# Dilated-attention values of two units of heads by seven block products instead of eight, with block sums made by transfers

## The chip, the cores and the metric

The kernel runs on one core of one Trainium2 chip. The metric is the device time of one execution in microseconds. Before the change it is 734.18 us, the median of three runs (733.82 to 734.69).

## The reference, cut to what matters

A four-layer encoder works on 256 tokens of width 1024, all in float32: an even layer (neighbourhood attention beside latent attention), an MLP, an odd layer (dilated attention), a second MLP. The change lies in the odd layer:

```python
def odd_mixer(xn, w_in, w_o, cos_f, sin_f):
    hcat = (xn @ w_in).reshape(b, s, DIL_GROUPS, 3, DIL_HEADS, HEAD_DIM)   # 3 groups; q, k, v; 16 heads of 64
    q = apply_rope(hcat[:, :, :, 0], cos_f, sin_f)
    k = apply_rope(hcat[:, :, :, 1], cos_f, sin_f)
    v = hcat[:, :, :, 2]
    return dilated_attention(q, k, v) @ w_o
```

Each head attends in three groups of keys (steps 1, 4 and 16), and the three results are mixed by their softmax denominators. Only the way in which `v` is computed changes, and with it one addition of the rotary embedding.

## The kernel before

**Precision.** A float32 matrix is carried as two parts of the type float32r: `hi` is the value cast by ScalarE, `lo` the remainder, taken by VectorE (`split`, L205 and L206). A product is three matmuls, hi·hi, hi·lo and lo·hi (`mm3`, L209 to L211).

**Weights.** One list, `specs`, holds every piece of weight in the order in which it is used. `weight()` (L196) gives the next piece; before that it lets `load_weight` run 4 pieces ahead (a transfer from SP into one of 4 rotating buffers `raw`, L151) and `split_piece` 2 pieces ahead (casts into `whi` by ScalarE and remainders into `wlo` by VectorE, in parts of a piece; 3 buffers of each). In the MLPs one block of a piece is a sum: GpSimd (POOL) copies a block and issues a transfer that adds two more blocks of HBM to it in SBUF (L144, L145).

**The odd layer.** The 16 heads are taken as 8 units of two heads. A unit has three pieces for queries and keys (`w_oqk`, 1024 KB each) and two for the values of its three groups (`w_ov`, 768 KB each). `qk_steps` makes 12 steps: step (b, f, half) is 8 matmuls of a 512-column and a 256-column form (L927, L928). After each f ScalarE and VectorE clear the bank (L934, L935); after each b follows the rotary embedding (`rope`, L939): four transfers on SP swap 32-row blocks into `sw` (L942), VectorE multiplies twice (L947, L948) and adds (L950 for b = 0; L953 for b = 1 and 2, into `q12` and `k12`). `all_values` then makes the values in 4 steps: two halves of 128 tokens times two halves of the width, 48 matmuls of 128x384, whose results VectorE (L904, into `v0`) and ScalarE (L907, L908, into `v12`) scale out of PSUM.

**What sets the order.** `weave` (L220) writes one unit's steps (main) and, spread between them, the attention of the unit before it (side): its scores (L218, L981), softmax (L992 to L997), four transposes of the probabilities (L1004, L1006), and the `mix` of the unit before that (L1019, L1024). From unit 2 on this is the loop at L1043. A scheduler that runs when the program is built then orders each engine's queue, and may take a split or a matmul of a later step first. Every queue runs in its order: an instruction that waits holds up all that stand behind it on its engine. Four PSUM banks are called `acc` and four `w`.

Of the kernel before, what the change touches and what calls it, by code (L numbers as in the profile page):

```python
# [43 lines left out]
WPARTS = 4  # L45
NORM_PRIO = 300
# [3 lines left out]
def trunk(ctx, tc, a, out):  # L50
# [54 lines left out]

    specs = []

    def plan(name, n):
        for j in range(a[name].shape[0]):
            specs.append((a[name][j], n, WPARTS, False))  # L110

    def plan_mlp(layer):
        up = [(a["w1"][layer, j], WCH, 2, False) for j in range(16)]
        down = [(a["w2"][layer, j], WCH, 2, j < 14) for j in range(16)]
# [19 lines left out]
    state = {"loaded": 0, "split": (0, 0), "used": 0, "pool": None, "parts_done": None}  # L134

    def load_weight(pieces=1, before=lambda i: None):
        j = state["loaded"]
        src, n, _, seven = specs[j]
# [8 lines left out]
        raw = wraw.tile([P, WCH], F32, tag="raw", name="raw")  # L147
# [5 lines left out]
        state["loaded"] = j + 1  # L153
# [5 lines left out]
    def split_piece(eng=None):  # L159
        j, i = state["split"]  # L160
        _, _, n, seven = specs[j]
# [11 lines left out]
        return split(hi, lo, raw, eng)  # L173
# [116 lines left out]
    def column(r, t):  # L290
        return r[:, t:t + 1]
# [578 lines left out]
    def odd(op, xT, s, late):  # L870
# [15 lines left out]
        def value_steps(d):  # L886
# [15 lines left out]
            def out(i):  # L902
                pq, ri = acc[i], column(r[0], i)
                nc.vector.tensor_scalar(d["v0"][:, i, :], pq[:, 0:P], ri, None, ALU.mult)  # L904
                for c in range(2):
                    rows = slice(64 * c, 64 * c + 64)
                    nc.scalar.activation(d["v12"][64:P, 2 * i + c, :], pq[rows, P:2 * P], AF.Copy, scale=ri[rows])  # L907
                    nc.scalar.activation(d["v12"][0:64, 2 * i + c, :], pq[rows, 2 * P:3 * P], AF.Copy, scale=ri[rows])  # L908

            return [lambda i=i, h=h: gemm(i, h) for i in range(NT) for h in range(2)], [lambda i=i: out(i) for i in range(NT)]  # L910

        def qk_steps(d, wide=True):
# [26 lines left out]
            def rope(b, pq):  # L939
# [6 lines left out]
                sw = sw.rearrange("p (f n) -> p f n", f=2)  # L946
                nc.vector.tensor_tensor(r1, pq.rearrange("p (f n) -> p f n", f=2), cosT.unsqueeze(1).broadcast_to([P, 2, T]), op=ALU.mult)  # L947
# [208 lines left out]
```

## Time and profile before

| | |
|---|---|
| median of three runs | 734.18 us |
| the profiled execution | 734.39 us, its span 732.6 us |
| TensorE (PE) busy | 723.4 us, 99% |
| VectorE (DVE) busy | 623.7 us, 85% |
| ScalarE (ACT) busy | 521.8 us, 71% |
| GpSimd (POOL) busy | 75.8 us, 10% |
| granted clock of TensorE, mean | 0.999 |
| units 1 to 7 of the odd layer begin at | 315.0, 343.4, 373.6, 403.3, 433.0, 462.7 and 492.5 us |

Times count from the start of the span. A row of a group ends with its busy time, the mean of one instruction in ns, and the idle time of its engine just before such instructions with what ended it. A row of a list in order of time begins with start and duration in us; back-to-back instructions overlap, so the spacing of two starts is what one costs its engine. A stage's row gives its length and then for each engine the busy time in it.

### The profile page before, as it was taken

Reading aid. Unit: us, or ns where it says so; the run is one execution under the profiler, and the core shown is the slowest. Engines: PE = TensorE matmul, PEld = TensorE weight load, DVE = VectorE, ACT = ScalarE, POOL = GpSimd, SP = SyncE. Lnnn points to the kernel's source line nnn. Section 1 sums busy time; section 2 is a strip of 40 time slices with the busy share of each in tenths; the row PEclk is TensorE's granted clock in tenths of the full one; section 3 lists DMA queues with packets and bytes.
Section 4 is the critical chain, followed back from the end, with each engine's and each line's share of the span. In section 5 each row is a group of like instructions: output and inputs, shape, how many; then the busy total and the mean of one; then the engine's idle time right before and its main releaser. Section 6 shows DMA issues by size and latency. Waiting matters only on the chain.

```text
span 732.6 us, 13831 instructions
## 1 busy us (share of the span) xinstructions
PE 723.4 (99%) x5234; PEld 661.0 (90%) x5234; DVE 623.7 (85%) x1188; ACT 521.8 (71%) x985; POOL 75.8 (10%) x73
## 2 busy tenths in 40 slices
PE   9999999999999999999999999999999999999995
PEld 6988899999999998989899899998999999999995
DVE  6888859999999959988777888788759998999956
ACT  7778968767767756877676766867658766776851
POOL 0100002224212000000000000000003132222000
PEclk9999999999999999999999999999999999999999
DMA  8773338799888644664655456455558797898601
GB/s 314 278 260 135 116 115 216 214 283 249 264 265 231 218 160 166 216 211 149 223 181 176 167 187 212 167 187 200 204 190 201 242 271 217 259 272 241 217 32 59
DMA packets 38212, 149.56 MB, mean 204 GB/s; under 512 B 5121, under 2 KB 6657, under 8 KB 29057
## 3 DMA queue, kind: packets, MB, share of 16 engines
q1 hardware_dynamic: 30240, 133.71, 51.6%
q0 software_dynamic: 7616, 14.68, 12.1%
q8 instruction: 41, 0.67, 0.4%
q10 hardware_dynamic: 288, 0.28, 0.1%
q14 instruction: 27, 0.21, 0.1%
HBM read 142.10 MB, written 1.05 MB: 195 GB/s over the span
## 4 chain that ended last, share of the span: by engine, by line
PE 82%; issue 10%; DVE 4%; ACT 1%; DMA 1%; POOL 0%; POOLq 0%; ACTq 0%; DVEq 0%
PE acc L927 11%; PE acc L209 10%; PE acc L210 9%; PE w L209 9%; PE w L210 9%; PE acc L211 9%; PE w L211 9%; PE acc L928 5%; PE w L218 1%; PE w L1004 1%; DVE wlo L206 1%; PE acc L1019 1%; PE w L806 1%; DMA sum<-in_w 1%; PE w L820 1%
## 5 line engine op out<-in xcount | busy, mean ns | idle before, releaser
L206 DVE TENSOR_TENSOR wlo<-raw,whi 128x512 fp32r<-128x512 f32 (+3 forms) x360 | 297.3, 847 | 51.9 <-ACT whi L205 51.8
L205 ACT CAST whi<-raw 128x512 fp32r<-128x512 f32 (+3 forms) x360 | 253.5, 746 | 87.2 <-PE w L210 58.9
L210 PE MATMUL w<-xx,whi 128*128 128x256 f32 x528 | 149.6, 283 | 0.2
L211 PE MATMUL w<-xx,wlo 128*128 128x256 f32 x528 | 149.3, 283 | 0.0
L209 PE MATMUL w<-xx,whi 128*128 128x256 f32 x528 | 148.9, 283 | 0.0
L927 PE MATMUL acc<-xx,whi 128*128 128x512 f32 x336 | 122.1, 404 | 0.0
L210 PEld LDWEIGHTS w<-xx,whi 128*128 128x128 f32 x528 | 101.2, 192 | 1.7 <-DVE xx L246 0.6
L209 PEld LDWEIGHTS w<-xx,whi 128*128 128x128 f32 x528 | 101.0, 192 | 1.1
L211 PEld LDWEIGHTS w<-xx,wlo 128*128 128x128 f32 x528 | 101.2, 192 | 0.0
L928 PE MATMUL acc<-xx,wlo 128*128 128x256 f32 x336 | 94.4, 281 | 0.0
L144 POOL COPY sum<-sum 128x512 f32<-128x512 f32 x28 | 39.3, 1417 | 463.6 <-DMA sum<-in_w 406.6
L927 PEld LDWEIGHTS acc<-xx,whi 128*128 128x128 f32 x336 | 63.1, 188 | 14.2
L928 PEld LDWEIGHTS acc<-xx,wlo 128*128 128x128 f32 x336 | 63.5, 189 | 0.0
L209 PE MATMUL acc<-whi,xx 128*128 128x384 f32 (+2 forms) x160 | 55.9, 351 | 0.0
L210 PE MATMUL acc<-wlo,xx 128*128 128x384 f32 (+2 forms) x160 | 55.4, 346 | 0.0
L211 PE MATMUL acc<-whi,xx 128*128 128x384 f32 (+2 forms) x160 | 54.9, 343 | 0.0
L205 ACT CAST hh<-h 128x896 fp32r<-128x896 f32 (+1 forms) x32 | 28.9, 904 | 24.5 <-DVE h L382 23.7
L209 PE MATMUL w<-whi,hh 128*128 128x512 f32 (+1 forms) x108 | 42.1, 390 | 0.0
L210 PE MATMUL w<-wlo,hh 128*128 128x512 f32 (+1 forms) x108 | 41.5, 384 | 0.0
L211 PE MATMUL w<-whi,hl 128*128 128x512 f32 (+1 forms) x108 | 41.2, 382 | 0.0
L206 DVE TENSOR_TENSOR hl<-h,hh 128x896 fp32r<-128x896 f32 (+1 forms) x32 | 34.8, 1087 | 0.0
L206 DVE TENSOR_TENSOR suml<-sum,sumh 128x1024 fp32r<-128x1024 f32 x28 | 34.4, 1229 | 0.0
(232 smaller groups left out, 1545.6 us busy)
## 6 DMA issues: line engine op xcount, KB each, us to landing
raw<-in_w SPq DMA_DIRECT2D x36, 1024.0 KB, 5.5
raw<-in_w_oqk SPq DMA_DIRECT2D x24, 1024.0 KB, 4.9
raw<-in_w SPq DMA_DIRECT2D x28, 768.0 KB, 4.8
sum<-in_w POOLq DMA_DIRECT2D x28, 512.0 KB, 7.9
raw<-in_w_ov SPq DMA_DIRECT2D x16, 768.0 KB, 4.4
sum<-in_w SPq DMA_DIRECT2D x28, 256.0 KB, 5.9
sw<-qk SPq DMA_DIRECT2D x84, 64.0 KB, 2.4
raw<-in_w_oe SPq DMA_DIRECT2D x4, 1024.0 KB, 5.9
```

Source lines behind the costliest of these rows:

```text
L144: nc.gpsimd.tensor_copy(out=sums[:, 1, :], in_=sums[:, 0, :])
L205: a = nc.scalar.copy(hi, src).ins
L206: return a, (eng or nc.vector).tensor_tensor(lo, src, hi.bitcast(F32), op=ALU.subtract).ins
L209: nc.tensor.matmul(o, sh, mh, start=first, stop=False)
L210: nc.tensor.matmul(o, sh, ml, start=False, stop=False)
L211: nc.tensor.matmul(o, sl, mh, start=False, stop=last)
L218: nc.tensor.matmul(o[j], y[pb, 0, ts], z[pb, 1, :], start=n == 0, stop=n == 2)
L806: nc.tensor.transpose(pt[:, b * P:(b + 1) * P], pp[:, b // 2, (b % 2) * P:(b % 2 + 1) * P], ident)
L820: nc.tensor.matmul(pvo[64 * j:64 * j + 64, 0:P], v[:, kk, h * 64:(h + 1) * 64], pts[:, 2 * j + kk, :], start=kk == 0, stop=kk == NT - 1)
L927: nc.tensor.matmul(two(pq), wh[:, ws], xT[:, k], start=k == 0, stop=False)
L928: nc.tensor.matmul(pq[:, T:2 * T], wl[:, ws], xh[:, k, :], start=False, stop=k == KT - 1)
L1004: nc.tensor.transpose(pt[:, b * P:(b + 1) * P], pp[:, at:at + P], ident)
```

## The change

The units 2 to 7 are taken as three pairs (2, 3), (4, 5) and (6, 7). For a pair the values are a product of 2 x 2 blocks: two halves of the tokens, two halves of the width (even and odd blocks of 128 features), two units. Written plainly that is eight block products of 12 matmuls each. Now it is seven (`pair_values`): P1, Q7, P2 and Q6 in the even unit of a pair, and Q4, Q5 and Q3 at the end of the odd unit, with sums of blocks on both sides.

- The sums of the token side are made once (`combine`, four calls: two woven into unit 1, two into unit 2): four ACT copies of 128x256 in two calls, three VectorE subtractions and a split each, into `combh` and `combl`.
- The weights are now four blocks for each pair (`w_op`, 768 KB each, b11 to b22; the same numbers in another layout). The sums of the weight side are made by transfers that POOL issues and that add a block of HBM onto a buffer `raw`. One buffer is held for a pair: it is loaded with b12, gets b22 added (for Q7); once it has been split for Q7 it gets b11 added (for Q6), and once it has been split for that, b21 (for Q4). Q5's piece is b11 with b12 added. While this lasts the other pieces rotate through 3 buffers.
- Value pieces are split in 2 parts of 768 columns (before: 4 of 384), seven pieces to a pair instead of four.
- The seven results are combined in two SBUF tiles `t` and `v` and in PSUM: ScalarE copies one, VectorE does eight operations of 128x384 to a pair, four of them into a scratch `c`, from which ScalarE scales into `v0` and `v12` (`place`).
- In `rope` for b = 1 of units 1 to 7 the product goes straight into `q12`, and a transfer of POOL adds `sw` to it.

```diff
 VCH = 4 * 384                                   # new
     for u in range(8):
-        ov = [(a["w_ov"][u, j], 4 * 384, WPARTS, False) for j in range(2)]
+        if u < 2:
+            ov = [piece(a["w_ov"][u, j], VCH, WPARTS) for j in range(2)]
+        else:
+            b11, b12, b21, b22 = (a["w_op"][u // 2 - 1, f] for f in range(4))
+            ov = [piece(b11, VCH, 2), piece(b12, VCH, 2, add=b22, held=True, then=b11),
+                  piece(b21, VCH, 2), piece(None, VCH, 2, held=True, then=b21)] if u % 2 == 0 else \
+                 [piece(None, VCH, 2, held=True), piece(b11, VCH, 2, add=b12), piece(b22, VCH, 2)]
         specs.extend(oqk + ov if u else ov + oqk)
...
+    def raw_tile(j, held=False):
+        if not held:
+            state["raw"] = (state["raw"] + 1) % (RAWBUFS - (summed[0] <= j <= summed[-1]))
+        return wraw.tile([P, WCH], F32, tag=f"raw{RAWBUFS - 1 if held else state['raw']}", name="raw", bufs=1)
...
+        if held:
+            if src is None:
+                parts[j] = [state["held"], None, None]
+                return
+            state["held"] = raw_tile(j, True)
...
+        if add is not None:
+            nc.gpsimd.dma_start(raw[:, 0:n], add, accum_op=ALU.add)
...
-        return split(hi, lo, raw, eng)
+        done = split(hi, lo, raw, eng)
+        if i == n - 1 and then is not None:
+            nc.gpsimd.dma_start(parts[j][0][:, 0:width], then, accum_op=ALU.add)
+        return done
...
+        def combine(b):
+            g, e = scratch([4, P], "g"), scratch([4, P], "e")
+            for f in range(2):
+                k = 2 * b + f
+                nc.scalar.activation(g[:, 2 * f:2 * f + 2, :], x[:, k, :].rearrange("p (t n) -> p t n", t=2), AF.Copy,
+                                     scale=gains[:, 2 * KT + k:2 * KT + k + 1])
+            nc.vector.tensor_tensor(e[:, 2:4, :], g[:, 1:2, :].broadcast_to([P, 2, P]), g[:, 0:4:3, :], op=ALU.subtract)
+            nc.vector.tensor_tensor(e[:, 1, :], g[:, 0, :], e[:, 3, :], op=ALU.subtract)
+            nc.vector.tensor_tensor(e[:, 0, :], g[:, 2, :], e[:, 1, :], op=ALU.subtract)
+            split(*(z[:, b] for z in comb), e)
+
+        def pair_values(first):
+            t, v = (op.tile([P, 384], F32, tag=n, name=n, bufs=1) for n in ("pt", "pv"))
+            plain, sums = {"P1": (0, 0), "P2": (1, 0), "Q4": (1, 1)}, {"Q3": 0, "Q6": 1, "Q7": 2, "Q5": 3}
+            def product(n):
+                wh, wl = weight()
+                pq = bank("acc")[:, 0:384]
+                for b in range(KT // 2):
+                    ws = slice(b * 384, b * 384 + 384)
...
+                    mm3(pq, a_h, a_l, wh[:, ws], wl[:, ws], b == 0, b == KT // 2 - 1)
+                return pq
+            def place(d, i, pq, other, op):
+                c = scratch([384], "c")
+                nc.vector.tensor_tensor(c, pq, other, op=op)
+                nc.scalar.activation(d["v0"][:, i, :], c[:, 0:P], AF.Copy, scale=column(r[0], i))
+                strided_values(d, i, c)
+            def p1():
+                nc.scalar.copy(t, product("P1"))
+            def q7():
+                nc.vector.tensor_tensor(v, product("Q7"), t, op=ALU.subtract)
+            def p2():
+                place(first, 0, product("P2"), t, ALU.add)
+            def q6():
+                pq = product("Q6")
+                nc.vector.tensor_tensor(t, pq, t, op=ALU.subtract)
+                nc.vector.tensor_tensor(v, pq, v, op=ALU.add)
...
+            return [p1, q7, p2, q6], lambda second: [q4, lambda: q5(second), lambda: q3(second)]
...
+                if b == 1 and wide:
+                    r1 = d["q12"]
...
+                elif b == 1 and wide:
+                    nc.gpsimd.dma_start(r1, sw, accum_op=ALU.add)
...
+        main[4:4], main[10:10] = [lambda: combine(0)], [lambda: combine(1)]
...
+            if u % 2 == 0:
+                now, later = pair_values(nd)
+            else:
+                now = later(nd)
+            weave(main + now, side + [lambda: mix(6, d, "acc")] if u == 7 else side)
```

Three places show how the queues change. **POOL between the two MLPs**, before (`rstd` belongs to the norm ahead of the odd layer, `sum` to the MLPs):

```order
L145 DMA sum<-in_w 128x2x512
L269 TENSOR_TENSOR rstd<-ms,mhalf 128x2
L144 COPY sum<-sum 128x512
L145 DMA sum<-in_w 128x2x512
L144 COPY sum<-sum 128x512 x2
```

and now, from unit 1 to unit 4 (L180 is a sum of a piece that is being loaded, L203 one that follows a split; `raw_4380` is the held buffer of the first pair, `raw_5183` of the second; `raw_4786` is Q5's piece):

```order
L300 TENSOR_TENSOR rstd_3578<-ms_3582,mhalf_92 128x2
L1057 DMA q12_3463<-sw_4014 128x512
L180 DMA raw_4380<-in_w_op 128x1536
L203 DMA raw_4380<-in_w_op 128x1536
L1057 DMA q12_4204<-sw_4449 128x512
L203 DMA raw_4380<-in_w_op 128x1536
L180 DMA raw_4786<-in_w_op 128x1536
L180 DMA raw_5183<-in_w_op 128x1536
L1057 DMA q12_4629<-sw_4852 128x512
L203 DMA raw_5183<-in_w_op 128x1536
L1057 DMA q12_5022<-sw_5243 128x512
```

POOL had nothing to do in the odd layer and now issues 19 adding transfers there: 4 to a pair and 7 of `q12`.

**VectorE in unit 2**, after the softmax of unit 1, before (`qk` clears an `acc` bank, `pts` takes transposed probabilities):

```order
L206 TENSOR_TENSOR wlo<-raw,whi 128x384
L947 TENSOR_TENSOR r_4333<-qk,cosT 128x512
L935 TENSOR_TENSOR qk<-acc,low 128x256
L206 TENSOR_TENSOR wlo<-raw,whi 128x384 x2
L1006 COPY pts<-w 128x384
L935 TENSOR_TENSOR qk<-acc,low 128x256
L206 TENSOR_TENSOR wlo<-raw,whi 128x384 x3
```

and now (with what each row waits for; `DMASW` is a transfer of POOL):

```order
L1037 TENSOR_TENSOR qk_4222<-acc_4334,low_4360 128x256 [waits Activation_49]
L958 TENSOR_TENSOR e_4344<-g_4343,e_4344 128x128 [waits DVE_49]
L959 TENSOR_TENSOR e_4344<-g_4343,e_4344 128x128 [waits DVE_49]
L237 TENSOR_TENSOR wlo_4523<-raw_4380,whi_4522 128x768 [waits DMASW7_49,PE_49,Activation_49]
L237 TENSOR_TENSOR combl_3454<-e_4344,combh_3453 128x512 [waits Activation_49]
L1051 TENSOR_TENSOR r1_4364<-qk_4222,cosT_3443 128x512
L1037 TENSOR_TENSOR qk_4393<-acc_4394,low_4411 128x256 [waits Activation_49]
L237 TENSOR_TENSOR wlo_4523<-raw_4380,whi_4522 128x768
```

The split of the held buffer waits for a sum by POOL and stands ahead of the row that clears the bank `acc_4394` of the queries.

**SP in unit 2**, before (`sw` are the swaps of the rotary embedding):

```order
L151 DMA raw<-in_w_oqk 128x2048 x2
L942 DMA sw<-qk 32x512 x4
L151 DMA raw<-in_w_oqk 128x2048
L942 DMA sw<-qk 32x512 x4
L151 DMA raw<-in_w_ov 128x1536
L942 DMA sw<-qk 32x512 x4
```

and now (unit 2 and the first loads of unit 3):

```order
L178 DMA raw_4549<-in_w_oqk 128x2048
L178 DMA raw_4380<-in_w_op 128x1536
L178 DMA raw_4571<-in_w_oqk 128x2048
L1044 DMA sw_4363<-qk_4222 32x512 x4
L1044 DMA sw_4449<-qk_4393 32x512 x4
L1044 DMA sw_4513<-qk_4466 32x512 x4
L178 DMA raw_4600<-in_w_oqk 128x2048
L178 DMA raw_4786<-in_w_op 128x1536
L178 DMA raw_4861<-in_w_op 128x1536
```

The loads of a unit stood one by one between the swaps; now they stand in groups ahead of and behind them. The held buffer is the fourth `raw`, so its load waits until the third piece of queries and keys of unit 2, which lay in it, has been split.

More of the change, by code (lines that the diff above doesn't have):

```diff
@@ L45 @@
 WPARTS = 4
+VCH = 4 * 384
 NORM_PRIO = 300
@@ L106, in trunk, with piece @@
     specs = []
+    def piece(src, n, parts, seven=False, add=None, held=False, then=None):
+        return src, n, parts, seven, add, held, then
     def plan(name, n):
         for j in range(a[name].shape[0]):
-            specs.append((a[name][j], n, WPARTS, False))
+            specs.append(piece(a[name][j], n, WPARTS))
     def plan_mlp(layer):
-        up = [(a["w1"][layer, j], WCH, 2, False) for j in range(16)]
-        down = [(a["w2"][layer, j], WCH, 2, j < 14) for j in range(16)]
+        up = [piece(a["w1"][layer, j], WCH, 2) for j in range(16)]
+        down = [piece(a["w2"][layer, j], WCH, 2, j < 14) for j in range(16)]
         specs.extend(up[:3])
@@ L146, in load_weight @@
             n = 3 * BLK
-        raw = wraw.tile([P, WCH], F32, tag="raw", name="raw")
+        raw = state["held"] if held else raw_tile(j)
         for i in range(pieces):
@@ L902, in out @@
             def out(i):
[L903 to L908, printed above, removed]
-            return [lambda i=i, h=h: gemm(i, h) for i in range(NT) for h in range(2)], [lambda i=i: out(i) for i in range(NT)]
+                nc.vector.tensor_scalar(d["v0"][:, i, :], acc[i][:, 0:P], column(r[0], i), None, ALU.mult)
@@ new lines, in out, with strided_values @@
+                strided_values(d, i, acc[i])
+            return [lambda i=i, h=h: gemm(i, h) for i in range(NT) for h in range(2)], [lambda i=i: out(i) for i in range(NT)]
+        def strided_values(d, i, v):
+            ri = column(r[0], i)
+            for c in range(2):
+                rows = slice(64 * c, 64 * c + 64)
+                nc.scalar.activation(d["v12"][64:P, 2 * i + c, :], v[rows, P:2 * P], AF.Copy, scale=ri[rows])
+                nc.scalar.activation(d["v12"][0:64, 2 * i + c, :], v[rows, 2 * P:3 * P], AF.Copy, scale=ri[rows])
@@ new lines, in pair_values, with q4, q5, q3 @@
+        def pair_values(first):
[6 more added lines that the diff above has]
+                    ws = slice(b * 384, b * 384 + 384)
+                    if n in plain:
+                        f, i = plain[n]
+                        a_h, a_l = (z[:, 2 * b + f, tok(i)] for z in (xh, xl))
+                    else:
+                        a_h, a_l = (z[:, b, sums[n], :] for z in comb)
+                    mm3(pq, a_h, a_l, wh[:, ws], wl[:, ws], b == 0, b == KT // 2 - 1)
[15 more added lines that the diff above has]
+                nc.vector.tensor_tensor(v, pq, v, op=ALU.add)
+            def q4():
+                place(first, 1, product("Q4"), v, ALU.subtract)
+            def q5(second):
+                pq = product("Q5")
+                place(second, 1, pq, v, ALU.add)
+                nc.vector.tensor_tensor(t, pq, t, op=ALU.add)
+            def q3(second):
+                place(second, 0, product("Q3"), t, ALU.add)
+            return [p1, q7, p2, q6], lambda second: [q4, lambda: q5(second), lambda: q3(second)]
```

24 lines of the change are left out of this document (16 added, 8 removed).

## The prediction

> **What bounds the kernel now.** First the page's summary and its chain of waits.
>
> ```profile
> span 732.6 us, 13831 instructions
> PE 723.4 (99%) x5234; PEld 661.0 (90%) x5234; DVE 623.7 (85%) x1188; ACT 521.8 (71%) x985; POOL 75.8 (10%) x73
> PE 82%; issue 10%; DVE 4%; ACT 1%; DMA 1%; POOL 0%; POOLq 0%; ACTq 0%; DVEq 0%
> ```
>
> TensorE holds the end, so matmuls taken out count in full as long as nothing else becomes the longer queue. Whether something does is read by stage: units 1, 2, 4 and 5 as they are now, and most of the second MLP.
>
> ```profile
> core 0: us, PE busy (x) PEld busy (x) DVE busy (x) ACT busy (x) POOL busy (x), PEclk, DMA share, GB/s
> 315.00:343.36 28.36, 28.36 (x203) 25.66 (x201) 24.70 (x61) 21.25 (x49) 0.00 (x0) 1.00 0.54 173
> 343.36:373.56 30.20, 30.20 (x234) 27.27 (x233) 24.09 (x62) 20.80 (x50) 0.00 (x0) 1.00 0.60 202
> 403.29:433.01 29.72, 29.72 (x233) 27.06 (x233) 24.40 (x62) 21.36 (x51) 0.00 (x0) 1.00 0.56 186
> 433.01:462.74 29.73, 29.73 (x234) 27.06 (x233) 24.40 (x62) 21.36 (x51) 0.00 (x0) 1.00 0.55 184
> 560.00:700.00 140.00, 140.00 (x938) 129.31 (x937) 131.64 (x169) 100.98 (x127) 29.01 (x22) 1.00 0.80 240
> ```
>
> In a unit TensorE is full and VectorE has 5.3 us of 29.7 to spare. In the MLP VectorE works 94% of the time, beside adding transfers of POOL, and TensorE still never waits. The change spends VectorE's spare time; the question is how much of it.
>
> **TensorE.** Three pairs lose 12 matmuls of 128x384 each. The end of unit 3 shows what one costs:
>
> ```profile
> 402.59 0.33 PE L211 MATMUL acc<-whi,xx 128*128 128x384 f32 x1
> 403.11 0.33 PE L211 MATMUL acc<-whi,xx 128*128 128x384 f32 x1
> 403.29 0.39 PE L927 MATMUL acc<-xx,whi 128*128 128x512 f32 x1
> 403.63 0.39 PE L927 MATMUL acc<-xx,whi 128*128 128x512 f32 x1
> ```
>
> The first two rows are three matmuls and 0.52 us apart, so one takes 0.173 us whatever its own duration says (and a pair of the forms for queries and keys, the last two rows, 0.34). 36 x 0.173 = 6.2 us less. An even unit keeps its 48 and its 29.7 us, an odd one falls to 36 and 27.6 us; a pair falls from 59.45 to 57.4 us.
>
> **VectorE, per pair.** Prices of its rows, from one unit's length (405.50 to 435.22 us) and, for the 1024 columns, from the MLPs:
>
> ```profile
> L206 DVE TENSOR_TENSOR wlo<-raw,whi 128x512 fp32r<-128x512 f32 x13 | 8.6, 686 | 3.2 <-ACT whi L205 3.2
> L206 DVE TENSOR_TENSOR wlo<-raw,whi 128x384 fp32r<-128x384 f32 x8 | 4.2, 552 | 0.0
> L935 DVE TENSOR_TENSOR qk<-acc,low 128x256 f32<-128x256 f32 x6 | 2.5, 418 | 0.1
> L1006 DVE COPY pts<-w 128x384 f32<-128x384 f32 x2 | 1.1, 554 | 0.4 <-PE w L1004 0.4
> L904 DVE TENSOR_SCALAR v<-acc,rstd 128x128 f32<-128x128 f32 x2 | 0.7, 346 | 0.0
> L996 DVE RECIPROCAL drz<-dz 128x1 f32<-128x1 f32 x4 | 0.6, 162 | 1.4 <-ACT pp L995 1.4
> ...
> L206 DVE TENSOR_TENSOR suml<-sum,sumh x28: 1209/1214/1630, 126.4 to 694.9; 128x1024 fp32r<-128x1024 f32 x28
> ...
> 428.43 1.29 DVE L206 TENSOR_TENSOR wlo<-raw,whi 128x512 fp32r<-128x512 f32 x2
> 429.64 0.35 DVE L904 TENSOR_SCALAR v<-acc,rstd 128x128 f32<-128x128 f32 x1
> ```
>
> Two splits of 512 start 1.21 us before the next row, 0.605 us each against a duration of 0.686: 0.08 us overlap. Less that, 384 columns cost 0.47 us, and 768, midway between 686 and 1214 ns, 0.87 us. Splits of values: 14 x 0.87 = 12.2 instead of 16 x 0.47 = 7.5 us, 4.7 more. Results: eight operations of 384 columns at 0.47 (the row of `pts`, which also reads PSUM) instead of four of 128 at 0.27 us, 2.7 more. The two additions into `q12` go, 1.2 less. Together 6.2 us more: 48.8 becomes 55.0 us of 57.4, 96%. By unit 28.3 of 29.7 and 26.6 of 27.6 us. `combine` comes on top, 0.34 + 2 x 0.27 + 0.61 = 1.5 us a call, two calls each in units 1 and 2. Unit 1 then has 24.7 + 3.0 - 0.6 = 27.1 us of 28.4 and fits; unit 2 has 28.3 + 3.0 = 31.3 us and does not fit its 29.7.
>
> **ScalarE.** Its casts of 384, 512 and 1024 columns, and the copy of a 128x384 result, set the price:
>
> ```profile
> L205 ACT CAST whi<-raw 128x512 fp32r<-128x512 f32 x13 | 7.3, 618 | 0.9 <-PE acc L927 0.8
> L205 ACT CAST whi<-raw 128x384 fp32r<-128x384 f32 x8 | 3.7, 514 | 1.4 <-PE acc L927 1.4
> L1006 ACT COPY pts<-w 128x384 f32<-128x384 f32 x2 | 1.0, 480 | 2.6 <-PE w L1004 2.6
> ...
> L205 ACT CAST sumh<-sum x28: 1036/1048/1059, 120.5 to 693.2; 128x1024 fp32r<-128x1024 f32 x28
> ```
>
> With 0.1 us overlap 768 columns cost 0.73 us: 14 x 0.73 - 16 x 0.41 = 3.6 us more, and four scalings and a copy about 1.8. 42.7 becomes 48.1 us of 57.4, 84%: costed at nothing, hidden beside VectorE's and TensorE's longer queues. Were VectorE shorter, it would still lie under TensorE by 9 us.
>
> **The adding transfers.** The MLPs' give the price, unit 4 that of a plain load.
>
> ```profile
> L145 POOL DMA_DIRECT2D sum<-in_w x28: 1087/1087/1688, 109.6 to 673.1; - x28
> DMA to landing us min/median/max: 6.4/7.9/12.2
> ...
> q1 hardware_dynamic: 4848, 23.86, 54.3%
> q0 software_dynamic: 2985, 5.77, 29.4%
> ...
> q1 hardware_dynamic: 1291, 5.48, 55.5%
> raw<-in_w_ov SPq DMA_DIRECT2D x2, 768.0 KB, 4.3
> ```
>
> The first pair is 512 KB from issue to landing; the second the queues from 560 to 680 us, 120 us: adding moves 5.77 MB in 35.3 us of all 16 engines, 163 GB/s, plain loads 366 GB/s. So a sum of 768 KB lands 1.6 us later than one of 512, after 8.0 to 9.5 us. With the wait for the split ahead of it, a cast (0.73) and a split (0.87) behind it, a sum between two products takes 10 to 11.5 us.
>
> Where is that covered? *Q7 to Q6 in units 4 and 6:* the order has the held buffer split between the first two clearings of the queries, and four halves of queries and keys (8 x 0.34 = 2.7 us each), P1, Q7 and P2 (2.1 each) stand on TensorE until Q6. That is 17 us, covered. *Q6 to Q4:* VectorE has about 13 us of splits and softmax in its own queue first, covered. *Q5:* its buffer comes free when unit 3's first piece has been split; load 4.3, sum 8.0 to 9.5 and cast make 13 to 14.5 us, VectorE's rows in between about 13. A wait of 0 to 1.5 us, with the clearing of two banks queued behind it. *The first pair:* the held buffer's load waits for the last split of unit 2's third piece. Then 4.3 + 0.4 + 8.0 to 9.5 + 0.73 = 13.4 to 14.9 us pass, and VectorE's rows up to that split take an estimated 9 us at the prices above (softmax 3, two splits of P1 1.7, the rest additions, clearings and copies). VectorE stands 4 to 6 us; the clearing of `acc_4394` is queued behind, P1 needs that bank, and unit 2 has no spare time to make it up. Q6's sum starts as late.
>
> The 4 us are a bound from below of VectorE's wait; of TensorE's, zero is, if its banks carry it over. From above it is the wait and unit 2's surplus, 6 + 1.6. I take 4.5 us for unit 2. For the three pairs: from below 0, as in the MLP at 94%; from above all of VectorE's 5.3 us stay idle, 55.0 + 10.6 = 65.6, 8.2 over TensorE's 57.4. The softmax's waits remain (1.4 a unit above), those of 3.2 for ScalarE's casts are a lead and go. I take 1.2 us a pair, nearest to the lower bound: 55.0 + 2.8 and up to 1.5 for Q5 is 57.8 to 59.3 us.
>
> **Sum** against the profiled execution's own 734.39 us: -6.2 + 3 x 1.2 + 4.5 = +1.9. The median is 0.2 us lower, so 736.1 us.
>
> **Rivals.** *The splits stay ahead.* Queues of 96% suffice, as 94% do in the MLP, and only unit 2's surplus of 1.6 us remains: 734.2 - 6.2 + 1.6 = 729.6 us. For it speaks the MLP's row; against it that there all sums are asked for well ahead, here a split has to end before its sum is begun.
>
> *The DMA engines become the bound.* A pair has 0.555 x 59.45 = 33.0 us of them now. A fifth plain block adds 2.1, four sums at 163 GB/s 19.3, two additions to `q12` 3.2: 57.6 us in 57.4. If rows of 6 KB cost by their bytes like the MLPs' rows of 2 KB, the stage cannot hold its pace: at 95% a pair takes 60.6 us, 1.2 over the present, and with unit 2's 4.5 the time is 734.2 + 3.5 + 4.5 = 742.2 us. If a sum costs like a load, the share is 78% and this falls away. For it speaks q0's rate, against it the buffers: nothing in the MLP was held up at 0.80 to 0.84.
>
> *POOL's issues are held up.* The row has 28 issues at 1087 ns, the worst 1688, with VectorE at 94%. Twelve sums 0.6 us later, three of four on a path, would add 5.4 us at most: 741.5 us. The Trainium skill ("SBUF — State Buffer", section "SBUF: two separate sides") warns of this: GpSimd cannot write the descriptors of its transfers while VectorE runs a float32 copy within SBUF. By that rule the sums would be late; the trace's 1087 in minimum and median shows no sign of it.
>
> That the matmuls do not go is no rival: the order has 36 fewer.
>
> **Chances.** Forecast 0.50 (own range 734.0 to 739.5), the splits stay ahead 0.26, the DMA engines 0.17, POOL's issues 0.03, VectorE's idle time all kept (750 and over) 0.04. About 0.2%, 1.5 us, is what this kernel's measurement can tell from no change. The second case is faster throughout (0.25), a third of the forecast and little else lies within (0.21), the rest is slower: 0.54. From 730.0 to 742.5 us some 2 in 10 are left out, half of the second case's low side and the tails above.
>
> **What would show it.** TensorE busy about 6 us less, and idle time of 7 to 9 us, most of it from unit 2's P1 to its Q6, with VectorE or ScalarE waiting for a transfer of `w_op` there; VectorE near 96% in units 3 to 7; sums landing in 8 to 9.5 us. If TensorE is full in units 4 to 7, the stalls per pair were mis-sized and the splits stay ahead; if landings go over 11 us and loads wait, it is the DMA engines. Wrong at the root would be a stall of TensorE outside units 1 to 7.

## The result: 4.5% slower

| | before | changed |
|---|---|---|
| median of the runs on one chip | 734.04 us (733.82 to 734.69, 4 runs) | 773.6 us (764.16, 770.51, 776.68, 780.55) |
| ratio | | 1.0452, 95% interval 1.0377 to 1.0526 |
| profiled execution, its span | 734.39, 732.6 us | 764.16, 761.9 us |
| granted clock of TensorE, mean | 0.999 | 0.989 (0.975 to 0.989) |

The ratio leaves out executions more than 1.5% over a kernel's shortest, here the two longest. The forecast was 736.1 us within 730.0 to 742.5: the side is right, the size far off.

The summary and the chain of waits of the changed kernel's page:

```profile
span 761.9 us, 13906 instructions
...
PE 731.9 (96%) x5198; PEld 659.6 (87%) x5198; DVE 647.5 (85%) x1204; ACT 542.4 (71%) x1005; POOL 93.9 (12%) x92
...
PE 79%; DVE 7%; DMA 7%; ACT 3%; issue 2%; SPq 1%; POOL 0%; POOLq 0%; DVEq 0%; ACTq 0%
```

TensorE has 36 matmuls fewer, yet stands 30.0 us where it stood 9.2, and transfers make 7% of the chain where they made 1%. Its busy time has grown by 8.5 us instead of falling by 6.2. Of these 14.7 us up to 6.8 are matmuls at half clock (below); e9, which has no such stretch in the odd layer, is still 4.3 us over (721.5 us busy), and where that comes from stays open. Before 315 us the two traces agree, and behind 575 us the changed one takes 186.9 us, as the one before does behind 545.7 us; the loss lies in units 1 to 7 and the scores behind them. TensorE's waits there (315 to 575 us; total, number, longest, us):

```profile
PE acc L241 <- DVE wlo L237: 9.1, 5, 2.8
PE acc L1029 <- DVE qk L1037: 3.1, 3, 1.0
PE w L1087 <- DMA q<-sw: 3.0, 1, 3.0
PE acc L240 <- ACT whi L236: 1.9, 1, 1.9
PE acc L1029 <- ACT whi L236: 1.3, 1, 1.3
PE w L1087 <- DVE k L1059: 1.3, 1, 1.3
```

They fall in every unit, not in unit 2 alone. What ScalarE and VectorE waited for from transfers (315 to 560 us):

```profile
ACT whi L236 <- DMA raw<-in_w_op: 13.1, 5, 3.9
...
DVE sw L1052 <- DMA sw<-qk: 9.5, 7, 2.8
```

And the transfers of that time, POOL's queue (packets, MB, share of the 16 engines) and three issues (number, KB each, median us from issue to landing):

```profile
q0 software_dynamic: 2736, 11.27, 26.5%
...
raw<-in_w_op POOLq DMA_DIRECT2D x12, 768.0 KB, 7.6
sw<-qk SPq DMA_DIRECT2D x84, 64.0 KB, 3.5
q<-sw POOLq DMA_DIRECT2D x7, 256.0 KB, 3.5
```

The sums land as soon as forecast or sooner (6.9 to 8.7 us). But casts wait 13.1 us for them, and the small swaps of the rotary embedding, 2.4 us before, now take 3.5 in the median and up to 7.9. The chain of waits shows how one becomes a wait of TensorE:

```profile
406.47 6.69 DMA sw<-qk
413.16 0.03 issue
413.19 0.05 DVEq L1052
413.24 0.04 issue
413.28 0.69 DVE sw L1052
413.98 0.88 DVE wlo L237
414.86 0.04 issue
414.90 0.69 PE acc L241
```

POOL had issued the sum for Q7 of the next pair at 405.52 us; it landed at 413.53. The swap issued 0.95 us behind it landed at 413.16, VectorE waited for it, and the split behind that row came 2.8 us late for TensorE. After such waits TensorE's clock falls; the windows are cut at the ends of the two first such stretches (length, PE, PEld, DVE, ACT, POOL, then the clock, the share of the DMA engines and GB/s):

```profile
360.00:377.20 17.20, 14.91 (x84) 12.91 (x82) 11.33 (x24) 9.68 (x21) 0.86 (x1) 1.00 0.75 189
377.20:384.00 6.80, 5.78 (x21) 4.80 (x21) 6.80 (x12) 6.51 (x14) 1.72 (x2) 0.50 0.69 188
384.00:414.80 30.80, 27.07 (x208) 23.17 (x207) 22.78 (x55) 19.19 (x41) 1.99 (x3) 1.00 0.82 218
414.80:418.20 3.40, 3.30 (x10) 3.30 (x11) 3.40 (x7) 1.94 (x5) 0.59 (x1) 0.50 1.04 332
```

Three stretches of 6.8, 3.4 and 3.4 us (the third from 452.3 us) cost up to 6.8 us here; in the other three runs the mean clock of 0.975 to 0.981 makes 14 to 19 us, worked out as (0.999 - clock) x span.

Units 4 and 5, which the prediction took as its pair:

```profile
420.00:454.00 34.00, 31.83 (x223) 27.57 (x223) 27.44 (x61) 25.23 (x54) 2.58 (x3) 0.98 0.72 206
454.00:487.50 33.50, 29.61 (x229) 25.29 (x228) 25.73 (x60) 20.86 (x47) 2.58 (x3) 0.97 0.86 233
```

67.5 us instead of 59.45. VectorE works 53.2 of them (forecast 55.0), ScalarE 46.1 (48.1), and VectorE stands 14.3 us where it stood 10.6. (Measured from the same matmul of both pairs, 420.00 to 488.06 us, the pair is 68.1 us long and VectorE works 53.7 of them.)

### The profile page after: what moved, and what is told of

Same layout as the page of the kernel before. It is cut to its first block, busy times and chain, and to the rows that moved or that the text cites. A ratio compares the mean times of both kernels' runs of the same rounds, so it can differ in the third digit from the quotient of the medians.

```text
span 761.9 us, 13906 instructions
## 1 busy us (share of the span) xinstructions
PE 731.9 (96%) x5198; PEld 659.6 (87%) x5198; DVE 647.5 (85%) x1204; ACT 542.4 (71%) x1005; POOL 93.9 (12%) x92
## 4 chain that ended last, share of the span: by engine, by line
PE 79%; DVE 7%; DMA 7%; ACT 3%; issue 2%; SPq 1%; POOL 0%; POOLq 0%; DVEq 0%; ACTq 0%
PE w L240 11%; PE w L241 11%; PE w L242 11%; PE acc L240 10%; PE acc L241 10%; PE acc L242 9%; PE acc L1029 6%; PE acc L1030 3%; DMA sw<-qk 3%; DVE wlo L237 3%; DMA raw<-in_w_op 2%; ACT whi L236 1%; SPq L1044 1%; PE w L249 1%; DMA q<-sw 1%
## 5 line engine op out<-in xcount | busy, mean ns | idle before, releaser
L237 DVE TENSOR_TENSOR wlo<-raw,whi 128x512 fp32r<-128x512 f32 (+4 forms) x354 | 310.9, 898 | 43.4 <-ACT whi L236 42.6
L236 ACT CAST whi<-raw 128x512 fp32r<-128x512 f32 (+4 forms) x354 | 266.4, 787 | 112.9 <-PE w L241 66.0
L171 POOL COPY sum<-sum 128x512 f32<-128x512 f32 x28 | 41.0, 1479 | 241.8 <-DMA sum<-in_w 185.7
L240 PE MATMUL acc<-whi,xx 128*128 128x384 f32 (+2 forms) x100 | 35.3, 356 | 1.1 <-DVE qk L1037 1.1
L241 PE MATMUL acc<-wlo,xx 128*128 128x384 f32 (+2 forms) x100 | 35.2, 352 | 0.3 <-DVE wlo L237 0.2
L242 PE MATMUL acc<-whi,xx 128*128 128x384 f32 (+2 forms) x100 | 34.7, 347 | 0.0
```

Source lines behind the costliest of these rows:

```text
L171: nc.gpsimd.tensor_copy(out=sums[:, 1, :], in_=sums[:, 0, :])
L236: a = nc.scalar.copy(hi, src).ins
L237: return a, (eng or nc.vector).tensor_tensor(lo, src, hi.bitcast(F32), op=ALU.subtract).ins
L240: nc.tensor.matmul(o, sh, mh, start=first, stop=False)
L241: nc.tensor.matmul(o, sh, ml, start=False, stop=False)
L242: nc.tensor.matmul(o, sl, mh, start=False, stop=last)
```

## The experiments

Ratios are to the kernel before on the same chip.

| kernel | median us | ratio (95% interval) |
|---|---|---|
| changed | 773.6 | 1.0452 (1.0377 to 1.0526) |
| e1 no sums | 755.77 | 1.0290 (1.0258 to 1.0323) |
| e2 sums of 16 columns | 754.88 | 1.0280 (1.0264 to 1.0297) |
| e3 sums unread | 771.88 | 1.0500 (1.0455 to 1.0545) |
| e4 plain transfers | 755.82 | 1.0274 (1.0245 to 1.0304) |
| e5 changed, q12 on VectorE | 775.16 | 1.0549 (1.0530 to 1.0568) |
| e6 small sums, q12 on VectorE | 750.93 | 1.0231 (1.0215 to 1.0246) |
| e7 before, q12 by transfer | 735.57 | 1.0022 (1.0010 to 1.0034) |
| e8 as e5, sums in thirds | 780.68 | 1.0633 (1.0562 to 1.0704) |
| e9 as e6, VectorE relieved | 737.62 | 1.0043 (1.0026 to 1.0060) |
| e10 as e6, splits in four | 745.18 | 1.0149 (1.0134 to 1.0164) |
| e11 before, splits in two | 734.02 | 0.9999 (0.9990 to 1.0008) |
| e12 before, subtraction twice | 744.31 | 1.0136 (1.0121 to 1.0151) |
| e13 changed, VectorE relieved | 758.80 | 1.0332 (1.0296 to 1.0367) |
| e14 changed, splits in four | 767.47 | 1.0453 (1.0397 to 1.0508) |
| e15 as e14, Q7's sum far later | 806.64 | 1.0981 (1.0965 to 1.0998) |
| e16 as e14, Q7's sum later | 767.11 | 1.0449 (1.0427 to 1.0472) |
| e17 as e16, q12 on VectorE | 769.71 | 1.0465 (1.0437 to 1.0492) |

### Are the sums to blame? (e1 to e4)

The first theory, from the trace: the sums make the stalls. Rival: queues of 96% on VectorE are too full by themselves.

e1, in `load_weight` and `split_piece`:

```diff
-        if add is not None:
-            nc.gpsimd.dma_start(raw[:, 0:n], add, accum_op=ALU.add)
-        if i == n - 1 and then is not None:
-            nc.gpsimd.dma_start(parts[j][0][:, 0:width], then, accum_op=ALU.add)
```

> The changed kernel without its twelve adding transfers of weights: every product reads plain blocks (the values come out wrong), the rest and its order stay. Theory A, the sums' transfers make the stalls (casts wait for them, and the swaps of queries and keys that are issued behind them land late): TensorE's waits of 3.7 us (unit 2), 2.9 (unit 3), 2.5 (unit 4), 2.9 (unit 5) and 1.5 us (unit 6) go, and with them the stretches at half clock (about 7 us in the profile of 764.2): 738 to 744 us, clock 0.998. Theory B, VectorE's and ScalarE's queues of 96% and 84% are too full by themselves: stalls remain in units 3 to 7, 752 us or more. The prediction's rival, the splits stay ahead, put such a kernel at 729.6 us.

Measured: 755.8 us, in the rival's range (752 us or more), and yet well below the changed kernel: both have a part. Some 12 to 18 us are the sums' (by ratio and by median), 21 us are not. Neither the 738 of the one nor the 729.6 of the prediction's rival was near.

e2:

```diff
-            nc.gpsimd.dma_start(raw[:, 0:n], add, accum_op=ALU.add)
+            nc.gpsimd.dma_start(raw[:, 0:16], add[:, 0:16], accum_op=ALU.add)
-            nc.gpsimd.dma_start(parts[j][0][:, 0:width], then, accum_op=ALU.add)
+            nc.gpsimd.dma_start(parts[j][0][:, 0:16], then[:, 0:16], accum_op=ALU.add)
```

> The twelve sums add 16 of 1536 columns (8 KB instead of 768 KB; the values come out wrong): each split still waits for its sum and each sum for its split, but hardly a byte moves. Theory A1, what stalls is bytes (landing times of 7 to 8.5 us, and swaps behind them): within 3 us of the kernel without sums, a sum lands in about 2 us. Theory A2, the chain split, issue, sum, cast, split itself is too long whatever it moves: 5 us or more above the kernel without sums, with TensorE waiting in units 2, 4 and 6 and not in 3 and 5.

Measured: 754.9 us, as without sums. Transfers of e2 from 315 to 545 us, and TensorE's waits there:

```profile
sw<-qk SPq DMA_DIRECT2D x84, 64.0 KB, 2.0
...
raw<-in_w_op POOLq DMA_DIRECT2D x12, 8.0 KB, 3.1
```
```profile
PE w L1087 <- DMA q<-sw: 6.1, 2, 3.0
PE acc L1029 <- DVE qk L1037: 3.1, 3, 1.0
```

The chain of split, sum and split costs nothing while no bytes move, and the swaps are as quick as before. The waits that are left are others: the scores wait for `q12`'s transfer, and the clearing of a bank comes late.

e3, the held buffer's sums keep their places but three products split a resident tile:

```diff
+        if specs[j][5]:
+            raw = state["xh"][:, 3 * i:3 * i + 3, :]
...
         done = split(hi, lo, raw, eng)
...
-            nc.gpsimd.dma_start(parts[j][0][:, 0:width], then, accum_op=ALU.add)
+            s = nc.gpsimd.dma_start(parts[j][0][:, 0:width], then, accum_op=ALU.add)
+            tc.add_manual_dep(s.ins, done[1].name, ...)
```

> All twelve sums move their 768 KB and are issued behind the same splits, but the three products that used the held buffer split a resident tile instead (values wrong), so no cast waits for these sums (Q5's still does). Theory A1 in its contention form, sums delay the swaps: units 3 and 5 keep their waits of 2.9 us, units 2, 4 and 6 some of theirs, swaps land up to 8 us after issue, 750 us or more. Theory A2, only the chain counts: 738 to 744 us, as without sums.

Measured: 771.9 us, as dear as the changed kernel. So it is not the wait for these sums. But the run is no clean proof of the swaps' part: with nothing to wait for, sums for Q7 went out beside those for Q5, and two at once landed 11.3 and 12.4 us after issue, so that ScalarE waited up to 5.4 us for Q5's, which is still read.

e4, both transfers lose `accum_op=ALU.add` and nothing else changes:

```diff
-            nc.gpsimd.dma_start(raw[:, 0:n], add, accum_op=ALU.add)
+            nc.gpsimd.dma_start(raw[:, 0:n], add)
```

> The twelve transfers stay with their issue, waits and bytes, and the order of every engine is the same, but they overwrite and do not add (values wrong). If the adding is what is dear (one lands after 7 to 8.5 us, a plain load of 768 KB after 4.3 to 5.0): landings of about 4.5 us, swaps behind them at most 5 us, 742 to 750 us. If any transfer of 768 KB more in these places delays the swaps enough: 755 us or more, near the changed kernel.

Measured: 755.8 us, as without any. Its waits and transfers, 315 to 550 us:

```profile
DVE sw L1052 <- DMA sw<-qk: 10.8, 4, 4.9
...
ACT whi L236 <- DMA raw<-in_w_op: 2.3, 2, 1.8
```
```profile
q0 software_dynamic: 2734, 11.27, 17.1%
...
raw<-in_w_op POOLq DMA_DIRECT2D x12, 768.0 KB, 5.7
```

The same bytes in the same order of every engine: the queue takes 40 us of all 16 engines (17.1% of 235) instead of 65 (26.5% of 245), a transfer lands after 5.7 instead of 7.6 us, and the casts wait 2.3 instead of 13.1 us. By the four runs of each (1.0274 and 1.0452) it is the adding that is dear, not a transfer more. That VectorE's waits for swaps stayed (10.8 us) hints that the swaps alone don't make the 12 to 18 us, and no more: e4's traced execution is its longest (761.67 us), the changed kernel's its shortest (764.16 us), so the two traces are only 2.5 us apart.

### The other 21 us: q12's transfer? (e5 to e8)

e5 and e6 take the branch out of `rope`, so that VectorE adds again; e6 has e2's sums too. e7 puts that branch alone into the kernel before. e8 is e5 with sums in three transfers.

```diff
-                elif b == 1 and wide:
-                    nc.gpsimd.dma_start(r1, sw, accum_op=ALU.add)
```
```diff
+            for q in range(0, n, BLK):
+                nc.gpsimd.dma_start(raw[:, q:q + BLK], add[:, q:q + BLK], accum_op=ALU.add)
```

> The changed kernel with one part undone: the second addition of the rotation into q12 is VectorE's again and no transfer of POOL; the sums stay. Theory Q: the scores wait for that transfer (in the kernel without sums it landed 8.0 us after issue behind two loads, and the five waits of the scores came to 11.9 us): 758 to 766 us, no wait of L1087's scores over 1 us, the waits behind the sums stay. Rival, VectorE's 96%: with 0.6 us a unit more on VectorE the time does not fall, 771 us or more.

> Sums of 16 columns (values wrong) and q12's addition on VectorE: neither of the two kinds of adding transfers is left. Theory Q with theory A1: 754.9 us less the scores' 11.9 us and some 5 us of half clock, 735 to 741 us, TensorE's waits only the three of 1.1 us behind the transposes and a few small ones. Rival, VectorE's and ScalarE's queues and the order are too full by themselves: 748 us or more.

> The kernel before with only this part of the change: q12's second addition is an adding transfer of 256 KB, no seven products, no sums. Theory Q: it is a cost of its own, since it lands 3.3 to 8 us after its issue where VectorE took 0.7 us, and the scores stand at the head of TensorE's queue: waits of 1 to 3 us in most units, 741 to 752 us. Rival: it only hurts where the pairs' order and sums have made q and k late; the kernel before has room: 733 to 736 us.

> As the kernel with q12 on VectorE, but each sum goes as three adding transfers of 512 columns instead of one of 1536. In the trace of the changed kernel no packet of a swap moved while the 128 packets of a sum did. If the engines take up another queue between two transfers: swaps behind a sum land in 3 to 5 us instead of 6 to 8 and the time is 5 us or more below the kernel with whole sums. If they serve the adding queue until it is empty: the same time within 3 us or, with POOL's 0.86 us an issue twice more, slower.

Measured: e5 775.2, e6 750.9, e7 735.6, e8 780.7 us. Theory Q falls as the main cause: without the transfer 17 us are still left (e6), and alone in the kernel before it costs 1.6 us (0.22%). Without sums it costs 0.5 points (e2 to e6), 3.6 us; beside the sums taking it back gained nothing: by ratio the time is a point longer, by median 1.6 us, where single runs of the changed kernel lie 16 us apart. VectorE's waits for swaps went from 9.5 to 19.5 us, in traced executions of 764.16 and 778.67 us. Why it turns over there was not settled. In e8 the swaps issued within 2 us behind a transfer of a sum landed after 2.7 to 6.1 us, 5.0 in the median; behind the whole sums of e5 it was 1.9 to 7.1 us and 6.6. So swaps do get in between a sum's transfers, but the time is no shorter for it. The reading of the changed kernel's trace in this expectation was too strong: 32 packets of swaps moved there between 408.1 and 409.7 us, while the sum issued at 405.52 us moved its own from 407.2 to 412.8 us.

Units 4 and 5 of e6, where the only adding transfers left in the odd layer are the sums of 16 columns, then VectorE's waits in them:

```profile
406.40:440.00 33.60, 31.52 (x219) 27.18 (x219) 27.14 (x62) 24.72 (x53) 0.86 (x1) 0.95 0.54 180
440.00:473.00 33.00, 31.48 (x237) 26.77 (x236) 29.26 (x65) 23.55 (x52) 2.58 (x3) 1.00 0.56 180
```
```profile
DVE qk L1037 <- ACT low L1036: 4.2, 3, 1.7
DVE drz L1100 <- ACT pp L1099: 2.2, 2, 1.6
DVE pts L1110 <- PE w L1108: 1.9, 3, 1.1
DVE sw L1052 <- DMA sw<-qk: 1.5, 2, 0.8
```

66.6 us, and VectorE busy 56.4 of them, which is what the prediction had (55.0 and 1.2 for the additions into `q12`). Busy time was priced right; 10.2 us of standing still stay beside it, nearly as much as before the change, but for other reasons. Before, 6.4 of the 10.6 us were waits for ScalarE's casts; these are gone. Now VectorE waits 4.2 us for the copies of ScalarE (`low`) that stand ahead of its clearing of a bank, 2.2 us for exponentials, 1.9 us for transposes and 1.5 us for swaps.

### VectorE (e9 to e12)

e9 on e6, the subtraction of the second 768 columns left out; e10 on e6, 2 parts become 4; e11 and e12 on the kernel before:

```diff
-        done = split(hi, lo, raw, eng)
+        done = split(hi, lo, raw, eng) if n == 4 or width != VCH or i == 0 else nc.scalar.copy(hi, raw)
...
-                        mm3(pq, a_h, a_l, wh[:, ws], wl[:, ws], ...)
+                        mm3(pq, a_h, a_l, wh[:, ws], (wl if b < 2 else wh)[:, ws], ...)
```
```diff
-        return split(hi, lo, raw, eng)
+        done = split(hi, lo, raw, eng)
+        if specs[j][1] == 4 * 384 and j > first_ov:
+            return done[0], nc.vector.tensor_tensor(lo, raw, hi.bitcast(F32), op=ALU.subtract).ins
+        return done
```

> The kernel with small sums and q12 on VectorE (750.9 us), and of each block of values VectorE splits only the first 768 columns (the product takes the high part twice for the others; values wrong): 7 x 0.87 = 6.1 us a pair off VectorE, 50.3 of 57.4 us. In that kernel units 4 and 5 took 66.6 us, VectorE 56.4 of them. Theory B1, VectorE's own 56 us and the waits between its rows set the pace: a pair falls by about the 6.1 us, 731 to 738 us. Theory B2, the order and the round trips of the softmax set it, whatever VectorE has to do: 746 us or more.

> The kernel with small sums and q12 on VectorE, with each block of values split in four parts of 384 columns instead of two of 768. Theory B3, a split of 0.95 us on VectorE and a cast of 0.83 us on ScalarE stand in the way of the short rows that TensorE waits for (softmax, clearing of banks): 741 to 747 us. Theory B1: 14 x (2 x 0.47 - 0.87) = 1 us a pair more on VectorE, 751 to 756 us.

> The kernel before with its value weights split in two parts of 768 from unit 2 on, nothing else. B3: the long rows alone make TensorE wait, 738 us or more. B1: VectorE has less to do by 0.3 us a unit and 5.3 us to spare, 733.5 to 735.5 us.

> The kernel before with every subtraction of a value split done twice on VectorE from unit 2 on: 8 x 0.47 = 3.8 us a unit more, 28.2 of 29.7 us, 95%; TensorE's, ScalarE's and the transfers' work is unchanged. Theory B1: the waits of VectorE of the present units stay and come on top, 56.3 + 10.6 = 66.9 instead of 59.45 us a pair at most, 745 to 756 us. Theory B2, it was the pairs' order: TensorE stays full, 734 to 738 us.

Measured: 737.6, 745.2, 734.0 and 744.3 us. TensorE's longest waits in e6 (315 to 560 us):

```profile
PE acc L1029 <- DVE qk L1037: 5.2, 5, 1.0
PE w L1108 <- ACT pp L1101: 2.2, 3, 1.0
```

Units 4 and 5 of e9, then as long a stretch of e10:

```profile
409.08:438.50 29.42, 28.62 (x197) 25.63 (x197) 23.24 (x56) 25.16 (x55) 1.72 (x2) 1.00 0.51 164
438.50:469.80 31.30, 31.16 (x276) 27.77 (x280) 26.86 (x63) 22.75 (x51) 1.72 (x2) 1.00 0.66 217
```
```profile
404.94:467.60 62.66, 60.84 (x453) 52.30 (x453) 55.92 (x138) 49.59 (x119) 3.44 (x4) 1.00 0.58 190
```

Two units of e12, and TensorE's waits from 315 to 560 us in it:

```profile
400.17:431.93 31.76, 30.19 (x233) 27.00 (x233) 27.77 (x69) 21.65 (x51) 0.00 (x0) 1.00 0.51 174
431.93:463.53 31.60, 30.03 (x232) 27.00 (x233) 27.77 (x69) 21.64 (x51) 0.00 (x0) 1.00 0.54 176
```
```profile
PE acc L214 <- DVE wlo L176: 7.4, 5, 1.6
```

| two units | length us | VectorE busy | VectorE idle |
|---|---|---|---|
| before | 59.45 | 48.8 | 10.6 |
| e9 | 60.7 | 50.1 | 10.6 |
| e10 | 62.7 | 55.9 | 6.7 |
| e12 | 63.4 | 55.5 | 7.8 |
| e6 | 66.6 | 56.4 | 10.2 |
| changed | 67.5 | 53.2 | 14.3 |

Theory B1 came out for e9: taking 6.1 us a pair from VectorE took 13.3 us off the time, though the matmuls, the transfers and ScalarE's work (47.9 us a pair) stayed. What TensorE lacked was room on VectorE and not the split that e9 leaves out: in e6 none of its waits is for a split. They are for cleared banks (5.2 us), for ScalarE's rows of the softmax and the transposes (3.2 us) and 1.1 us for others.

e12 points the same way, less surely. The kernel before, given 6.7 us a pair more on VectorE (7.5 by the row's price) at the same matmuls and transfers, became 10 us slower, with a wait of up to 1.6 us for a split in each unit. These waits are for the doubled split itself, so that a split that is merely late would fit as well.

e10 shows that VectorE's work is not all of it. Theory B3 had said 741 to 747 us and B1 751 to 756 us: with the same work, shorter splits took 6 us off. TensorE's waits for ScalarE's softmax and transposes fell from 3.2 to 0.2 us, and e6's stretch at half clock (3.4 us) is gone; the waits for cleared banks stayed (5.2 and 4.9 us). In the kernel before the length of the splits does nothing (e11). So the time that VectorE stands is no constant, 6.7 to 10.6 us in the rows without large sums; in the kernel before and in e9 TensorE works 59.5 and 59.8 us of the two units, and VectorE's idle time there is in part TensorE's doing.

### How the two act together (e13 to e17)

e13 is the changed kernel with e9's edit, e14 with e10's. e15 and e16 add to e14, where the held buffer is loaded and in `rope` (`s` in the last line is VectorE's row that takes up the swaps; `if b == 2` is in e16 only):

```diff
-            nc.gpsimd.dma_start(raw[:, 0:n], add, accum_op=ALU.add)
+            s = nc.gpsimd.dma_start(raw[:, 0:n], add, accum_op=ALU.add)
+            if held:
+                tc.add_manual_dep(s.ins, state["swapped"], ...)
...
+                if b == 2:
+                    state["swapped"] = s.ins.name
```

> The changed kernel, sums and q12's transfer as they are, but VectorE splits only the first 768 columns of each block of values (values wrong), 6.1 us a pair less. Theory C1, the two causes multiply: the sums' 18 us are only so dear because a VectorE at 96% cannot catch up after a late swap; with room it costs little: 737 to 745 us. Theory C2, they add: 773.6 - 13.3 = 760, so 756 to 764 us.

> The changed kernel with each block of values split in four parts of 384 instead of two of 768 columns, all else as it is. Without sums this took 5.7 us off. If the shorter rows let the softmax and the clearing through as there: 762 to 770 us. If with the sums the late swaps hide that: 771 to 778 us.

> As the changed kernel with splits in four, and the first sum of each pair (for Q7, asked for a unit early) is issued only when VectorE has taken up the last swap of the unit before it. In the changed kernel those sums, issued at 405.5 and 473.5 us, held up the swaps of units 3 and 5 and TensorE stood 2.8 us at 414.9 and at 484.5 us. Contention of sums and swaps: these two waits go, 5 us or more below the kernel with splits in four. If the sums cost where they are waited for: the same within 3 us, or slower because Q7's sum comes later.

> Splits in four, and the first sum of each pair (for Q7) issued only once VectorE has taken up the last swaps of the unit before the pair. In the run before this one the wait had been hung on the latest rotation written ahead of the load, which is the pair's own first one: the sum went out some 40 us later and TensorE waited 5 us and more for it and for what hangs on it. Here PE, VectorE, ScalarE and the loads' queue keep the order of the kernel with splits in four, only POOL's issues of those sums move, by some 8 us. Contention of sums and swaps: TensorE's waits of 5.0 us at 406.5 and 4.5 us at 475.7 us of that kernel go or fall below 1.5 us, and with them a stretch or two at half clock, 752 to 762 us where it took 767.5. If a sum costs the same wherever it goes: 765 to 772 us.

> The kernel before this one (splits in four, Q7's sum behind the last swaps of the unit before the pair) and q12's addition on VectorE again. There the waits behind the swaps had gone (VectorE waited 0.4 instead of 9.9 us for swaps), but q12's transfer, now beside two loads and that sum, landed 8.0 us after issue and the scores waited 3.3, 3.8 and 5.1 us for it. If those waits are what took its gain away: 12 us and 3 us of half clock less and 1.2 us a pair more on VectorE, 751 to 758 us, the best of the kernels that compute all. If VectorE's waits fill the gap again: 763 us or more.

Measured: 758.8, 767.5, 806.6, 767.1 and 769.7 us. e13: the causes add within the noise (theory C2). From e9 to e13 the sums and `q12`'s transfer cost 2.9 points, from e6 to the changed kernel 2.2, with an interval of 0.8 either side: room on VectorE does not hide them. Up to 10 us of e13 are half clock (20.5 us of it in its trace). e14: by ratio the splits in four gain nothing beside the sums, with an interval of 0.9 points either side, by median 6.1 us; so the 0.8 points of e10 are neither shown nor excluded there.

e15 hung the wait on the wrong rotation: it is the latest one written ahead of the load, the pair's own first. The sum for Q7 of the pair (4, 5) left at 454.3 us, behind that pair's own swaps, and TensorE stood for the casts behind it (315 to 600 us):

```profile
PE acc L242 <- ACT whi L238: 26.2, 6, 5.3
```

That says only what a late first sum costs: 39 us over e14. e16 does what was meant. The first row is e14's, of VectorE's waits, the second e16's; then TensorE's waits in e16 (all from 315 to 570 us):

```profile
DVE sw L1052 <- DMA sw<-qk: 9.9, 4, 4.0
```
```profile
DVE sw L1054 <- DMA sw<-qk: 0.4, 1, 0.4
```
```profile
PE w L1091 <- DVE wlo L239: 6.9, 2, 3.7
PE w L1091 <- DMA q<-sw: 5.1, 1, 5.1
```

The waits for swaps are gone, and the time is the same. The sum now travels beside the next loads and `q12`'s transfer (issued at 407.42, landed at 415.45 us), and the scores wait 3.2, 3.7 and 5.1 us instead. For the first two the profile names a split of VectorE, which scores don't read; `q12`'s transfer had landed 0.13 us ahead of the first. With `q12` on VectorE again (e17) those waits go too, and the time does not: VectorE then waits 6.2 us for swaps, 12.9 us for ScalarE's exponentials and 10.5 us for casts, and TensorE 6.3 us for cleared banks. No version here beats the kernel before.

## Why the prediction was wrong

- **TensorE, -6.2 us.** The 36 matmuls went; 0.173 us each was never contradicted. They would make 728.0 us.
- **VectorE's and ScalarE's prices** held within 2 us a pair (56.2 forecast and 56.4 measured for VectorE in e6, 48.1 and 48.3 for ScalarE).
- **"I take 1.2 us a pair, nearest to the lower bound": this term failed.** A pair was to take 57.8 to 59.3 us; with sums of 16 columns and `q12` on VectorE (e6) it took 66.6 us. VectorE's idle time was to fall to the softmax's 2.8 us, and it stayed at 10.2. The wait for ScalarE's casts went as forecast, but waits for the copies ahead of the clearing of banks, for transposes and for swaps took its place (4.2, 1.9 and 1.5 us), and the step had no term for them. Its upper bound, all of VectorE's 10.6 us of idle kept, said 65.6, and the case built on it (750 us and over) had been given 0.04. What misled was the row of the second MLP, 94% with TensorE full: there (560 to 700 us) VectorE waits 4.4 us for casts, 2.8 us for one load and 0.6 us for one other row of ScalarE, and TensorE never. In a unit it takes turns with ScalarE and TensorE in clearing and softmax. In ratios: 1.9 points, 13.8 us, fall away when VectorE is relieved by 6.1 us a pair (e6 to e9). e9 still lies 1.3 points, 9.3 us, over 728.0, and its three pairs make 3 x (60.7 - 57.4) = 9.9 us.
- **The sums.** Landing times were right, and the DMA engines were not the bound (0.78 of units 4 and 5). Missing was what a transfer does to others at that share: casts wait 13.1 us, swaps land up to 7.9 us after issue, and two sums at once take 11.3 and 12.4 us. The sum had no term for it; it is 1.7 points or 12.6 us, from e2 to the changed kernel, with an interval of some 5.6 us either side (18.7 us by the medians). That "Q7 to Q6" is covered by 17 us of TensorE was nearly so: in unit 4 the sum for Q6 landed at 445.40 us, and TensorE stood 0.55 and 1.5 us.
- **`q12`'s transfer** was priced in engine time alone, not in latency: it landed 3.3 to 9.2 us after issue, ahead of the scores, where VectorE took 0.7. It cost 3.6 us without sums and 1.6 us alone, and is not to be separated beside the sums.
- **Unit 2, 4.5 us.** The place was nearly right and the sum was another. The wait that was worked out, for the first sum (Q7's), was there, 2.6 us of ScalarE and 2.3 us of VectorE at 363 us, and TensorE did not wait for it. It stood 1.9 us ahead of Q6 and 1.3 us behind it, from 374.6 us on, after ScalarE had waited 3.9 us for the second sum with its other casts behind. That is 3.2 us, with the 3.4 us that the stretch at half clock behind it can cost 6.6; that 4.5 lies between them is in part luck.
- **The clock** was in no term. e9, e6, e2 and the changed kernel, profiled at 0.999, 0.994, 0.990 and 0.989, lose 0, 4, 7 and 8 us by (0.999 - clock) x span. These are contained in the shares below. The Trainium skill ("TensorE: Matmul & The Clock Gate", section "What's actually happening") says that TensorE falls to half rate after a window of about 3.4 us of idleness. Here shorter waits did it (below).
- **Rivals.** POOL's issues took 0.86 us each and held nothing up. The sign "VectorE near 96%" did not come: it works 79% of units 4 and 5. "Wrong at the root" was to be a stall outside units 1 to 7, and there is one: TensorE waits 3.0 us for unit 7's own scores, in the output product. Most of the loss lies inside the units all the same.

The shares, in points of the time before: -0.84 for the matmuls, +1.27 that e9 lies above that, +1.88 for VectorE's 6.1 us, +0.49 for `q12`, +1.72 for the sums: +4.52. They are the steps from one kernel to the next, so they add up by construction, and another order gives other shares: from the changed kernel to e13 VectorE's 6.1 us are worth 1.2 points, 0.8 either side. What stays open is how the sums' share is divided between late casts and late swaps: each wait that was taken away came back at another place.

## What to carry to other kernels

When an engine's idle time in a stage comes from round trips with other engines, do not count it as spare: the upper bound is the new work on top of the whole stage, idle included. Here 7.6 us more work a pair made the pair 7.2 us longer in e6, 3.2 to 4.0 us for about as much in e10 and e12, though VectorE had been busy only 82% of the time. A stage in which the same engine reaches 94% on work that runs ahead says little of it. Price a transfer by when it lands beside its neighbours and by whom it delays, not only by its share of the engines. Look at the granted clock once TensorE waits: in the changed kernel it made the waits dearer and the time scatter, in e12 waits of up to 1.6 us did not move it.

## What was not expected of the hardware

- **Half clock after short waits.** The granted clock was 0.50 for 3.4 or 6.8 us (10.2 in e5, e13 and e15, 13.7 in e17) after TensorE had waited 1.9 and 1.3 us close together, 2.8 us, or 0.55 and 1.5 us, and in e6 after only 0.98 and 1.04 us. After 2.85 us at 484.5 us and 2.96 us at 556.4 us it stayed at 1.00, and so it did in e12 after five waits of 1.2 to 1.6 us. At half clock the matmuls of 384 columns start 0.32 us apart instead of 0.173. It is not the same from run to run: the mean clock was 0.975 to 0.989 for one kernel. The Trainium skill ("TensorE: Matmul & The Clock Gate", section "What's actually happening") gives a window of 3.4 us that runs freely, not from the kernel's start. The lengths here, one to four times 3.4 us, agree; the trace adds that waits shorter than the window are enough.
- **An adding transfer is over 1.6 times as dear to the engines as a plain one** of the same rows (65 to 40 us for the same 11.27 MB of POOL's queue, of which 1.84 add in both kernels), and what is issued just behind it may wait for all of it: swaps issued at 474.1 us, 0.6 us behind a sum, landed 7.9 us later. Not each does: one issued 0.31 us behind the sum of 405.52 us landed some 2.7 us ahead of it. The Trainium skill ("DMA: Bandwidth & Descriptors", section "Queues, rings and completion order") says that an engine changes its queue only between packets of several descriptors. That swaps behind sums in thirds landed sooner in the median (5.0 instead of 6.6 us) agrees.
